# Seven products for eight in three quarters of an encoder's MLP, one core of a Trainium2 chip

## The chip, the core and the metric

The kernel runs on one core of a Trainium2 chip. The metric is the time of one execution on the device in microseconds (us). TensorE (PE) multiplies matrices into the banks of PSUM, VectorE (DVE) and ScalarE (ACT) work on tiles of 128 partitions, GpSimd (POOL) helps, and SyncE (SP) issues transfers (DMA).

## What is computed

Two layers of an encoder on 512 tokens of 1024 features, all in fp32:

```python
for l in range(DEPTH):
    sh1, sc1, gt1, sh2, sc2, gt2 = split(silu(c) @ ada_w[l] + ada_b[l], 6)
    h = rms_norm(x, norm1_g[l]) * (1.0 + sc1) + sh1
    ...
    x = x + gt1 * (merged @ w_out[l])
    h = rms_norm(x, norm2_g[l]) * (1.0 + sc2) + sh2
    x = x + gt2 * (square(relu(h @ w_mlp1[l])) @ w_mlp2[l])
```

What the dots leave out are the two branches of a layer, differential attention and a gated delta rule, with their gates. The last line, the MLP, is what the change is about: `w_mlp1` is 1024 x 4096, `w_mlp2` 4096 x 1024. Both layers have it.

## The kernel before, in words

**Layout.** x and everything dense is feature-major: a tile `xT[k]` holds 128 features (partitions) of all 512 tokens (free dimension), eight tiles for 1024 features. A dense product takes a block of weights of eight 128 x 128 tiles (`chunk`, L539: one load of 1024 values a partition, half a megabyte) and makes 128 output features: the weights stand still in PE, and 512 tokens move.

**Precision.** Every operand of a dense product is a high part, rounded to the format fp32r, and a low part, the difference (`split`, L556). Weights: a cast on ACT (`whi`), a subtraction on DVE (`wlo`), 1024 values a partition each. A product is three passes into one bank: high.high, low.high, high.low. `dense` (L715) does it for all tokens, `dense_halves` (L733) for the first 256 and then the other 256 tokens.

**The MLP** (L1303) goes by quarters of the 4096 hidden features. In each of the four quarters (L1306) the first product makes eight tiles of 128 hidden features: 8 blocks x 8 tiles x 3 passes = 192 matmuls of 512 columns (names `d_m1`; in a layer's first quarter four of the blocks go by halves of the tokens, `d_m1f`). `evac1` (L1309) takes each bank: relu and square on ACT, then the split into `uh` and `ul`. The second product again has 8 blocks x 8 tiles x 3 passes = 192 matmuls (`d_m2`), and `evac2` (L1320) adds each result, times its column of the modulation, to `xT` on DVE. The last quarter of layer 0 goes by halves, since the next layer's norm follows.

**The modulation** (`ada`, L631): each of its 48 columns a layer is a load of half a megabyte and one DVE operation of 1024 values that sums along the row. Those of layer 1 are done beside layer 0's MLP.

**The order.** The code takes operations down (`Plan`, L178); `schedule` (L250) then orders them for each engine by estimated times and five levels (chains, evacuations, weights, dense products, and last what stands beside, such as layer 1's columns), under limits of memory slots, and `issue` (L400) issues them. So every instruction shows line 417, and is known by its tiles. Constants such as the number of slots and of banks kept free stand at L421 and L465.

Of the kernel before, what the change touches and what calls it, by code (L numbers as in the profile page):

```python
# [10 lines left out]
F32 = mybir.dt.float32  # L11
# [17 lines left out]
# columns of the array of vectors  # L29
# [3 lines left out]
# columns of the constant array  # L33
# [31 lines left out]
class Tl:  # L65
    """A tile that gets its memory when its first writer is placed."""
# [14 lines left out]
def _rearrange(a, pat, sizes):  # L81
    """einops' rearrange of a numpy view, for splits, permutations and merges."""
# [27 lines left out]
class View:  # L110
    """A part of a tile: its extent as a numpy view, and the steps that lead to it."""
# [69 lines left out]
class Plan:  # L181
    """Takes down the operations of the kernel in program order, gives them an order by estimated times under the
    limits of memory, and issues them in it."""
# [11 lines left out]
    def add(self, engs, fn, args, kw):  # L195
# [14 lines left out]
        for w, vs in ((False, ins), (True, outs)):  # L210
            for v in vs:
# [20 lines left out]
        # VectorE and GpSimd take turns at their second port to SBUF  # L232
# [6 lines left out]
    def held(self, blocked, order):  # L239
        """What waits for memory, and what holds it."""  # L240
# [8 lines left out]
    # ------------------------------------------------------------------ order  # L249
    def schedule(self):  # L250
# [19 lines left out]
        def offer(op):  # L270
            """Memory for the op, if there is; then it is a candidate from its earliest time."""
# [42 lines left out]
        while todo:  # L314
# [28 lines left out]
            if e != "sp" and op.key[0] >= 0 and HOLD[int(op.key[0])] is not None:  # L343
                # not in the way of a more pressing operation that is about to be ready
# [6 lines left out]
            # two engines don't read one bank of PSUM at the same time  # L351
# [7 lines left out]
            if e == "pe":  # L359
                # TensorE's clock is halved after a window with little work  # L360
# [38 lines left out]
    # ------------------------------------------------------------------ issue  # L399
# [20 lines left out]
# estimates of times in ns, for the order alone  # L420
# [48 lines left out]
# the pieces of the two branches of each layer, in order: d projections of the delta rule, a b c its three parts,  # L469
# z its gate; q k v projections of the attention, t its heads  # L470
# [5 lines left out]
def encoder(ctx, tc, a, out):  # L476
    pl = Plan(tc, {"F": NF, "Y": NY, "Z": NZ, "B": 8},
              {"raw": KRAW, "whi": KHI, "wlo": KLO, "ada0": NADA, "ada": 2, "d": 3, "d0": ND0, "xTp": 1, "po": 2, "pv": 2, "sgf": LSG, "rawg": 1, "whig": 1, "wlog": 1, "dg": 1, "sga": 3, "sc": LSC})
# [24 lines left out]
    # ---------------------------------------------------------------- constants  # L503
# [32 lines left out]
    # ---------------------------------------------------------------- helpers  # L536
    loads = []

    def chunk(src, name, after=(), level=None, cls="F", grp="", wl=2):  # L539
        """A weight block [128, nk, n] of 1024 values a partition, as high and low part: views by k."""  # L540
        nk, n = src.shape[1:]
        per = nk if cls == "F" else nk // 2
        raw = F([P, nk, n], f"raw_{name}", grp="raw" + grp)
        his, los = ([pl.tile(cls, [P, per, n], f"{w}_{name}", F32R, grp=w + grp if cls == "F" else None)
# [16 lines left out]
    def rsqrt(dst, ss, scale):  # L561
        """dst = (ss * scale + eps) ** -0.5: a first guess from the exponent, three Newton steps."""
# [11 lines left out]
    def sumsq(dst, x, by_act):  # L574
        """dst[:, t] = sum of x[:, t]^2 along the row."""
# [10 lines left out]
    def acc(bank, i, lhsT, rhs, stop, level=CHAIN, after=()):  # L586
        """bank[:, i] += lhsT^T rhs: all products into a bank are one group, from the first to the one with stop."""
# [9 lines left out]
    def square(k, xk, hf):  # L597
        """Sums of squares of half of the tokens over the feature tiles of x: a running sum, the last tile for itself."""
# [9 lines left out]
    # ---------------------------------------------------------------- start  # L608
    # twice silu(c), in all partitions
# [6 lines left out]
    # one over the root mean square of x, token-major, on the diagonals of four matrices  # L616
# [33 lines left out]
    for l in range(DEPTH):  # L650
# [6 lines left out]
        # nlam = -(e0 - e1 + lam_init)  # L657
# [75 lines left out]
    def dense_halves(blocks, xh, xl, evac, name, after=()):  # L733
        """Blocks of weights [128, nk, 128], for the first half of the tokens and then for the second; evac(m, psum, half)."""
# [19 lines left out]
    # ---------------------------------------------------------------- the layers  # L754
    mid = []
    for l in range(DEPTH):
# [3 lines left out]
        # ---- per layer constants  # L760
# [19 lines left out]
        # ================================================= differential attention: q, k, v  # L780
# [3 lines left out]
        def da_dense(kind, j):  # L784
            """Columns of one block of two heads, token-major; two banks of two token tiles."""
# [50 lines left out]
        # ================================================= delta rule: projections  # L836
# [36 lines left out]
        # token-major scalars [128, dir, t, h]  # L873
# [4 lines left out]
        def ba_proj():  # L878
            # the high parts of the weights above the low parts: two passes give all products
# [10 lines left out]
            def evac():  # L890
# [9 lines left out]
                # beta = 1 / (1 + exp(-b))  # L900
# [3 lines left out]
                # g = -exp(A_log) * softplus(a + dt_bias)  # L904
# [4 lines left out]
                # log1p(y) = 2 atanh(y / (2 + y))  # L909
# [20 lines left out]
                # the sums as rows  # L930
# [75 lines left out]
            # the 32 x 32 diagonal blocks; partition = (head, unit, block), unit = (dir, chunk)  # L1006
# [21 lines left out]
        def gdn_b(h0, n, XA):  # L1028
            """Inverses of the diagonal blocks of heads h0 .. h0 + n - 1, all at once."""
# [36 lines left out]
            # X = D + N X with N = D L, in three steps; in step n the blocks n beside the diagonal and farther out  # L1066
            # become right, a corner of 4 - n blocks
# [18 lines left out]
            # the recurrence over chunks  # L1086
# [35 lines left out]
            # outputs  # L1122
# [278 lines left out]
```

## Time and profile before

| what | value |
|---|---|
| runs | 1668.42, 1670.18, 1670.42 us, median 1670.18 |
| the profiled execution's span | 1667.5 us |
| PE busy | 1638.8 us (98%), 9456 instructions |
| DVE busy | 1142.1 us (68%) |
| ACT busy | 757.6 us (45%) |
| POOL busy | 159.2 us (10%) |
| DMA | 232.47 MB, mean 139 GB/s |

The span is the profiled execution's own time from its first to its last instruction; the runs are timed by the device from outside, without a profile. Busy time of an instruction goes from its start to its end, and instructions of one engine overlap at their ends, so what one costs in a stream is the distance between two starts. A name such as `d_m` stands for all tiles whose names begin so, and loses its numbers.

### The profile page before, as it was taken

To read this page: it belongs to the slowest core of one execution; us is meant where nothing else is said; L and a number is where in the kernel's file an instruction comes from. 1 tells how busy PE (TensorE), PEld (TensorE's weight loads), DVE (VectorE), ACT (ScalarE), POOL (GpSimd) and SP (SyncE) were. 2 spreads that over 40 slices of the span, in tenths; PEclk is the share of its full clock that TensorE was granted. 3 is DMA by queue.
4 is the path that set the end of the run, shared out by engine and by line. 5 is a ranking of instruction groups with operands and counts; after the bars stand their busy time and mean duration, and the time that the engine had idled before them with its cause. 6 is when DMAs were issued, how large, how long until landed. Compare 5 with 4: busy or idle time off the path is not lost.

```text
span 1667.5 us, 25355 instructions
## 1 busy us (share of the span) xinstructions
PE 1638.8 (98%) x9456; PEld 1410.4 (85%) x9456; DVE 1142.1 (68%) x2653; ACT 757.6 (45%) x1474; POOL 159.2 (10%) x170
## 2 busy tenths in 40 slices
PE   7999999999999999999999999999999999999998
PEld 5889998878898888888998889768889988888887
DVE  7999797898888983333688987998637743333332
ACT  5653452575356252424557335555424652515150
POOL 0231140000300000000023112100002000000000
PEclk9999999999999999999999999999999999999999
DMA  9332534445667982332443332614244433323311
GB/s 379 133 107 96 189 115 146 120 114 186 226 216 265 340 326 90 102 100 90 134 146 113 135 101 72 151 59 126 76 145 139 137 104 101 99 91 101 99 53 51
DMA packets 96782, 232.47 MB, mean 139 GB/s; under 512 B 26625, under 2 KB 37505, under 8 KB 96658
## 3 DMA queue, kind: packets, MB, share of 16 engines
q1 hardware_dynamic: 96658, 230.84, 41.9%
q8 instruction: 74, 1.21, 0.3%
q14 instruction: 50, 0.41, 0.1%
HBM read 217.66 MB, written 13.14 MB: 138 GB/s over the span
## 4 chain that ended last, share of the span: by engine, by line
PE 83%; DVE 12%; DMA 2%; issue 1%; ACT 1%; POOL 0%; SPq 0%; DVEq 0%; ACTq 0%; POOLq 0%
PE d_m L417 39%; PE d_g L417 7%; PE d_dn L417 5%; PE d_out L417 5%; PE d_da L417 5%; PE d_m1f L417 3%; PE d_brb L417 3%; PE d_bra L417 2%; PE d_z L417 2%; PE px L417 2%; PE pv L417 2%; DVE XA L417 2%; DVE btmp L417 2%; PE po L417 1%; PE pog L417 1%
## 5 line engine op out<-in xcount | busy, mean ns | idle before, releaser
L417 PE MATMUL d_m<-uh,wlo_m 128*128 128x512 f32 (+1 forms) x576 | 210.5, 366 | 0.0
L417 PE MATMUL d_m<-ul,whi_m 128*128 128x512 f32 (+1 forms) x576 | 210.4, 365 | 0.0
L417 PE MATMUL d_m<-uh,whi_m 128*128 128x512 f32 (+1 forms) x576 | 210.4, 366 | 0.0
L417 ACT CAST whi_m<-raw_m 128x1024 fp32r<-128x1024 f32 x128 | 132.6, 1049 | 137.1 <-DVE wlo_m L417 70.1
L417 PE MATMUL d_m<-hh,whi_m 128*128 128x512 f32 x448 | 174.3, 389 | 0.0
L417 PE MATMUL d_m<-hl,whi_m 128*128 128x512 f32 x448 | 174.3, 389 | 0.0
L417 PE MATMUL d_m<-hh,wlo_m 128*128 128x512 f32 x448 | 174.3, 389 | 0.0
L417 DVE TENSOR_TENSOR wlo_m<-raw_m,whi_m 128x1024 fp32r<-128x1024 f32 x128 | 156.3, 1221 | 15.8 <-ACT whi_m L417 15.7
L417 DVE SCALAR_TENSOR_TENSOR xT<-d_m,mod,xT 128x512 f32<-128x512 f32 (+1 forms) x72 | 49.7, 690 | 166.5 <-PE d_m L417 166.4
L417 DVE TENSOR_TENSOR ul<-relu,uh 128x512 fp32r<-128x512 f32 x64 | 44.2, 691 | 162.6 <-ACT uh L417 162.6
L417 ACT ACTIVATE relu<-d_m 128x512 f32<-128x512 f32 x56 | 33.5, 598 | 218.8 <-PE d_m L417 218.8
L417 PEld LDWEIGHTS d_m<-ul,whi_m 128*128 128x128 f32 x576 | 108.6, 189 | 17.6
L417 PEld LDWEIGHTS d_m<-uh,wlo_m 128*128 128x128 f32 x576 | 108.6, 189 | 17.5
L417 PEld LDWEIGHTS d_m<-uh,whi_m 128*128 128x128 f32 x576 | 108.6, 189 | 17.4
L417 DVE SCALAR_TENSOR_TENSOR ada<-ada,cb 128x1024 f32<-128x1024 f32 x96 | 116.4, 1227 | 10.0 <-DMA ada<-in_ada_w_dram 8.4
L417 PE MATMUL d_da<-whi_da,hl 128*128 128x256 f32 x384 | 109.4, 287 | 0.0
L417 PE MATMUL d_da<-whi_da,hh 128*128 128x256 f32 x384 | 109.2, 287 | 0.0
L417 PE MATMUL d_da<-wlo_da,hh 128*128 128x256 f32 x384 | 107.5, 287 | 0.0
L417 PE MATMUL d_g<-hh,whi_g 128*128 128x512 f32 x256 | 103.7, 405 | 0.0
L417 PE MATMUL d_g<-hl,whi_g 128*128 128x512 f32 x256 | 103.1, 403 | 0.0
L417 PE MATMUL d_g<-hh,wlo_g 128*128 128x512 f32 x256 | 102.5, 400 | 0.0
L417 PEld LDWEIGHTS d_m<-hh,wlo_m 128*128 128x128 f32 x448 | 84.1, 188 | 17.5
(289 smaller groups left out, 4087.0 us busy)
## 6 DMA issues: line engine op xcount, KB each, us to landing
raw_m<-in_w_mlp_dram SPq DMA_DIRECT2D x128, 512.0 KB, 3.5
ada<-in_ada_w_dram SPq DMA_DIRECT2D x96, 512.0 KB, 6.2
raw_g<-in_w_g_dram SPq DMA_DIRECT2D x32, 512.0 KB, 5.2
raw_out<-in_w_out_dram SPq DMA_DIRECT2D x32, 512.0 KB, 4.3
raw_dn<-in_w_dn_dram SPq DMA_DIRECT2D x24, 512.0 KB, 6.0
raw_da<-in_w_da_dram SPq DMA_DIRECT2D x24, 512.0 KB, 3.9
raw_z<-in_w_dn_dram SPq DMA_DIRECT2D x8, 512.0 KB, 4.9
gb<-grow SPq DMA_DIRECT2D x16, 256.0 KB, 4.7
```

Of the source, the lines that this page charges most:

```text
L417: op.ins = getattr(eng[op.eng[0]], fn)(*[real(v) for v in op.args], **{k: real(v) for k, v in op.kw.items()})
```

## The change

In the first three quarters of each layer (`NSTR = 3`) the second product is cut into blocks, two by two by two: tokens in two halves of 256, the quarter's hidden features into even and odd tiles, output features into two halves of 512. By the scheme of Strassen in Winograd's form seven products of such blocks, with sums of blocks before and after, give what eight products gave. In the sums of u: t1 = o1 - o0 with o0, o1 and so on being pieces of even (e) and odd (o) tiles by halves of the tokens.

- `evac1` makes four differences of 256 tokens for each pair of hidden tiles (`u13`, `u24`) and splits e0 (256) and three tiles of 512 (`ule`, `ul24`, `ul13`, `ulo` are the low parts).
- The weights come in blocks of 512 output features (`load`), are summed in place (`m20` to `m23`, eight sums of 1024 values), and 14 of them are split (`m2hi`, `m2lo`).
- A product (`product`) is token-major: a piece of u stands still, 512 output features of weights move, into a pair of banks for two tiles of 128 tokens: 2 x 4 x 3 = 24 matmuls. Products p1, p6, p7 and p4 add up in one pair (`m2x`), p5 and p3 in another (`m2y`), p2 stands alone (`m2z`).
- `gather` copies or adds these sums into `y`, token-major, 14 times a quarter.
- x is saved to DRAM after the output projection. In the last quarter it is loaded again, y is transposed by PE (32 transposes of 128 x 128 a layer, `yT`), and one DVE operation a tile adds it, times the modulation, to x. The last quarter's second product is done as before.

The diff, cut to its core (comments are dropped throughout the file, and `w_m2` is `w_mlp2` in the new blocks):

```diff
+NSTR, LPLAIN, LSUMS, KEEPS = 3, 8, 8, 1
+G0, G1, G2, G3, G4, G5, GL, GM, GP, GQ = 7, 0, 0, 0, 0, 0, 0, 2, 6, 0
+GS, NYF, KEEPM = (3, 5), 2, (3, 2)
...
             square(m, xT[m], hf)
+            if hf:
+                sp.dma_start(out=xs[m], in_=xT[m], level=SIDE)
...
             def evac1(m, ps):
                 r = Y([P, S], "relu")
                 act.activation(r, ps, AF.Relu)
                 act.activation(r, r, AF.Square)
-                uh.append(Y([P, S], "uh", F32R))
-                ul.append(Y([P, S], "ul", F32R))
-                split(uh[-1], ul[-1], r)
...
+                r0, r1 = r[:, HALF[0]], r[:, HALF[1]]
+                p = m // 2
+                if m % 2 == 0:
+                    split(piece("e0", p, 0), piece("e0", p, 1), r0)
+                    sums = {n: Y([P, 2, S // 2], f"u{n}") for n in ("13", "24")}
+                    minus(sums["13"][:, 0], r1, r0)
+                    even.append((r1, sums))
+                else:
+                    e1, sums = even.pop()
+                    t1, t3, t2, t4 = (sums[n][:, i] for n in ("13", "24") for i in range(2))
+                    minus(t3, r1, e1)
+                    minus(t2, r1, t1)
+                    minus(t4, r0, t2)
+                    sums["o"] = r.rearrange("p (i s) -> p i s", i=2)
+                    for n in ("24", "13", "o"):
+                        split(uP[0][n][p], uP[1][n][p], sums[n])
...
+                for g in range(2):
+                    go = [begin[GS[g]]] + last
+                    a21, a11, a22, a12 = (load(ij, g, go, "sums", KEEPS) for ij in (2, 0, 3, 1))
+                    for dst, x_, y_, o_ in ((a11, a11, a21, ALU.subtract), (a21, a21, a22, ALU.add),
+                                            (a22, a22, a11, ALU.subtract), (a12, a12, a22, ALU.subtract)):
+                        dve.tensor_tensor(out=dst, in0=x_, in1=y_, op=o_, level=WGT)
...
+                p1 = product(plain(0, [begin[GP]] + last), "e0", X, before)
+                gather(X, 0, 0)
+                p6 = product(mixed(s2, [begin[G0]]), "t2", X)
+                gather(X, 0, 1)
+                p5 = product(mixed(s1, [p1[G1]]), "t1", Yq)
+                gather(Yq, 1, 1)
+                p7 = product(mixed(s3, [p6[G2]]), "t3", X)
+                gather(X, 1, 1)
+                p3 = product(mixed(s4, [p5[G3]]), "o1", Yq)
+                gather(Yq, 0, 1)
+                p4 = product(plain(3, [p5[G4]]), "t4", X)
+                gather(X, 1, 0)
+                p2 = product(plain(1, [p7[G5]]), "o0", Z_)
+                gather(Z_, 0, 0)
...
+            for m in range(NK):
+                sp.dma_start(out=xT[m], in_=xs[m], level=WGT, after=before)
+                ps = B([P, S], "yT", grp="m2", keep=KEEPB)
+                for t in range(NT):
+                    pe.transpose(ps[:, t * P:(t + 1) * P], (y[t][:, m // 4] if t < NYF else y[t][m // 4])[:, m % 4 * P:(m % 4 + 1) * P], ident, level=SIDE, after=before)
+                dve.scalar_tensor_tensor(out=xT[m], in0=ps, scalar=mod[l][:, 40 + m:41 + m], in1=xT[m], op0=ALU.mult, op1=ALU.add,
+                                         level=EVAC)
```

The order that this gives, at three places. First VectorE in layer 0, second quarter, at the end of the first product. Before (`ul` is the low part of a hidden tile, `ada1` a column of layer 1's modulation, `wlo_m1` the low part of a weight block of the first product):

```order
L417 TENSOR_TENSOR ul_6741<-relu_6722,uh_6735 128x512
L417 SCALAR_TENSOR_TENSOR ada1_32_6701,mod1_6201<-ada1_32_6701,cb_103 128x1024
L417 SCALAR_TENSOR_TENSOR ada1_33_6713,mod1_6201<-ada1_33_6713,cb_103 128x1024
L417 TENSOR_TENSOR wlo_m15_6765<-raw_m15_6600,whi_m15_6762 128x1024
L417 SCALAR_TENSOR_TENSOR ada1_34_6747,mod1_6201<-ada1_34_6747,cb_103 128x1024
L417 TENSOR_TENSOR ul_6788<-relu_6771,uh_6783 128x512
```

Now, up to the differences of the last pair of hidden tiles:

```order
L417 TENSOR_TENSOR m22_6933<-m22_6933,m23_6944 128x1024
L417 TENSOR_TENSOR ul24_7021<-u24_6995,uh24_7010 128x512
L417 TENSOR_TENSOR m23_6944<-m23_6944,m20_6937 128x1024
L417 TENSOR_TENSOR m21_6971<-m21_6971,m23_6944 128x1024
L417 TENSOR_TENSOR u13_7048<-relu_7032 128x256
L417 TENSOR_TENSOR ule_6959<-relu_7032,uhe_6947 128x256
L417 SCALAR_TENSOR_TENSOR ada1_14_6863,mod1_6475<-ada1_14_6863,cb_103 128x1024
L417 TENSOR_TENSOR m2lo_7065<-m20_6980,m2hi_7024 128x1024
L417 TENSOR_TENSOR m2lo_7076<-m20_6984,m2hi_7037 128x1024
L417 TENSOR_TENSOR u13_7048<-relu_7069,relu_7032 128x256
L417 TENSOR_TENSOR u24_7089<-relu_7069,u13_7048 128x256
L417 TENSOR_TENSOR ulo_7095<-relu_7069,uho_7086 128x512
```

Between two tiles of u there stand sums of weights and pieces of u where there were mostly columns; the last sum (`m21`) comes before the pieces of the last pair.

Then PE in layer 1, second quarter, where the second product passes from its first to its second block. Before (one block of weights to the next, whose results go to another bank):

```order
L417 MATMUL d_m2_15357<-uh_15330,whi_m21_15236 128x512
L417 MATMUL d_m2_15357<-ul_15335,whi_m21_15236 128x512
L417 MATMUL d_m2_15357<-uh_15330,wlo_m21_15239 128x512
L417 MATMUL d_m2_15389<-uh_15064,whi_m22_15274 128x512
L417 MATMUL d_m2_15389<-ul_15069,whi_m22_15274 128x512
L417 MATMUL d_m2_15389<-uh_15064,wlo_m22_15277 128x512
```

Now (from p1's last matmuls to p6's first; `uhe` and `ule` are e0's parts, `uh24` and `ul24` those of t2 and t4):

```order
L417 MATMUL m2x_15788<-m2hi_15738,ule_15655 128x512
L417 MATMUL m2x_15788<-m2lo_15758,uhe_15643 128x512
L417 MATMUL m2x_15763<-m2hi_15727,uh24_15516 128x512
L417 MATMUL m2x_15763<-m2hi_15727,ul24_15521 128x512
L417 MATMUL m2x_15763<-m2lo_15768,uh24_15516 128x512
L417 MATMUL m2x_15763<-m2hi_15727,uh24_15609 128x512
```

The piece of u stands still and the weights move, and p6 goes on in the bank `m2x_15763` that p1 filled 12 matmuls earlier.

Last PE in layer 1, last quarter, after the third block of the second product:

```order
L417 MATMUL d_m2_17068<-uh_17014,whi_m22_16958 128x512
L417 MATMUL d_m2_17068<-ul_17019,whi_m22_16958 128x512
L417 MATMUL d_m2_17068<-uh_17014,wlo_m22_16961 128x512
L417 MATMUL yT_17097<-cst_88,y0_15154 128x128
L417 MATMUL yT_17097<-cst_88,y1_15177 128x128
L417 MATMUL yT_17097<-cst_88,y20_15195 128x128
L417 MATMUL yT_17097<-cst_88,y30_15216 128x128
L417 MATMUL yT_17102<-cst_88,y0_15154 128x128
```

Here nothing stood before between the third and the fourth block; now all 32 transposes do, four into each bank.

## Rows read from the trace of the kernel before

**Rows 1.** The page: span, busy time of each engine, PE's clock in 40 slices

```profile
span 1667.5 us, 25355 instructions
...
PE 1638.8 (98%) x9456; PEld 1410.4 (85%) x9456; DVE 1142.1 (68%) x2653; ACT 757.6 (45%) x1474; POOL 159.2 (10%) x170
...
PEclk9999999999999999999999999999999999999999
```

**Rows 2.** The chain of waits, longest pieces: start us, us, what

```profile
948.52 8.65 PE d_da L417 x72
...
1295.50 16.67 PE d_out L417 x139
...
1336.81 326.44 PE d_m L417 x1440
```

**Rows 3.** Busy time by stage of layer 0's MLP

```profile
core 0: us, PE busy (x) PEld busy (x) DVE busy (x) ACT busy (x) POOL busy (x), PEclk, DMA share, GB/s
497.00:535.50 38.50, 38.50 (x235) 34.51 (x234) 33.73 (x59) 26.41 (x46) 0.00 (x0) 1.00 0.73 254
535.50:579.10 43.60, 43.60 (x194) 36.09 (x193) 39.31 (x62) 10.20 (x11) 0.00 (x0) 1.00 0.95 350
579.10:622.60 43.50, 43.50 (x193) 36.04 (x192) 37.74 (x62) 20.70 (x29) 0.00 (x0) 1.00 0.91 328
622.60:666.00 43.40, 43.40 (x193) 35.92 (x192) 15.10 (x16) 11.04 (x12) 0.00 (x0) 1.00 0.31 98
666.00:709.60 43.60, 43.60 (x194) 36.12 (x193) 15.31 (x16) 19.64 (x28) 0.00 (x0) 1.00 0.30 97
```

**Rows 4.** Timeline of VectorE in layer 0's MLP: start us, us, what

```profile
497.20 2.08 DVE L417 TENSOR_TENSOR xn<-xT,nrb 128x256 f32<-128x256 f32 x6 [0.42 <-PE nrb L417]
...
533.47 0.69 DVE L417 TENSOR_TENSOR ul<-relu,uh 128x512 fp32r<-128x512 f32 x1
534.07 1.22 DVE L417 SCALAR_TENSOR_TENSOR ada<-ada,cb 128x1024 f32<-128x1024 f32 x1
...
541.39 1.22 DVE L417 TENSOR_TENSOR wlo_m<-raw_m,whi_m 128x1024 fp32r<-128x1024 f32 x1
542.52 0.75 DVE L417 SCALAR_TENSOR_TENSOR xT<-d_m,mod,xT 128x512 f32<-128x512 f32 x1
543.19 1.22 DVE L417 SCALAR_TENSOR_TENSOR ada<-ada,cb 128x1024 f32<-128x1024 f32 x1
```

**Rows 5.** Instruction groups of VectorE, 497 to 622.6 us: busy us, mean ns, idle before

```profile
L417 DVE SCALAR_TENSOR_TENSOR ada<-ada,cb 128x1024 f32<-128x1024 f32 x53 | 63.6, 1220 | 10.0 <-DMA ada<-in_ada_w_dram 8.4 <-PE d_m L417 1.5
```

**Rows 6.** Timeline of ScalarE in layer 1's MLP

```profile
1342.31 0.60 ACT L417 ACTIVATE relu<-d_m 128x512 f32<-128x512 f32 x1 [2.60 <-PE d_m L417]
1342.94 0.63 ACT L417 ACTIVATE relu<-relu 128x512 f32<-128x512 f32 x1
1343.61 0.62 ACT L417 CAST uh<-relu 128x512 fp32r<-128x512 f32 x1
1344.13 1.05 ACT L417 CAST whi_m<-raw_m 128x1024 fp32r<-128x1024 f32 x1
```

**Rows 7.** Timeline of PE around four transposes of layer 1's attention

```profile
1194.28 0.60 PE L417 MATMUL oT<-cst,oa 128*128 128x128 f32 x4
1194.64 0.48 PE L417 MATMUL d_brb<-ybh,wlo_brb 128*128 128x512 f32 x1
1194.95 0.40 PE L417 MATMUL d_brb<-ybh,whi_brb 128*128 128x512 f32 x1
```

**Rows 8.** Busy time in three stretches at the start

```profile
5.00:10.00 5.00, 1.21 (x2) 0.00 (x0) 1.73 (x5) 5.00 (x10) 0.00 (x0) 1.00 1.03 405
10.00:15.00 5.00, 2.12 (x10) 2.12 (x11) 4.36 (x21) 0.13 (x2) 0.00 (x0) 1.00 1.03 407
20.00:25.00 5.00, 4.67 (x19) 3.24 (x18) 5.00 (x12) 3.37 (x6) 0.00 (x0) 0.68 1.03 410
```

**Rows 9.** Busy time over most of layer 1's branches

```profile
900.00:1200.00 300.00, 292.42 (x1934) 250.96 (x1934) 259.52 (x765) 157.15 (x381) 48.53 (x60) 1.00 0.34 98
```

More of the change, by code (lines that the diff above doesn't have):

```diff
@@ L542, in chunk @@
         per = nk if cls == "F" else nk // 2
-        raw = F([P, nk, n], f"raw_{name}", grp="raw" + grp)
-        his, los = ([pl.tile(cls, [P, per, n], f"{w}_{name}", F32R, grp=w + grp if cls == "F" else None)
+        kr, kh = KEEPM if name.startswith("m1") and name[2] != "f" else (0, 0)
+        raw = F([P, nk, n], f"raw_{name}", grp="raw" + grp, keep=kr)
+        his, los = ([pl.tile(cls, [P, per, n], f"{w}_{name}", F32R, grp=w + grp if cls == "F" else None, keep=kh)
                      for i in range(nk // per)] for w in ("whi", "wlo"))
@@ L1300, in evac_out, with piece, minus @@
             square(m, xT[m], hf)
+            if hf:
+                sp.dma_start(out=xs[m], in_=xT[m], level=SIDE)
         dense_halves(blocks("w_out", l, NK), mh, ml, evac_out, "out", [gate["a"]])
         h2h, h2l, normed = norm(l, 1, xT)
-        mid = [normed]
+        y, seen, before, late, last = [F([P, 2, 512], f"y{t}") if t < NYF else [Y([P, 512], f"y{t}{i}") for i in range(2)] for t in range(NT)], set(), [], [], []
+        xT = [Y([P, S], f"xT{k}") for k in range(NK)]
         for q in range(4):
-            uh, ul = [], []
+            halves, uh, ul = q < NSTR, [], []
+            if halves:
+                uE = [[Y([P, 2, S // 2], f"{w}e", F32R) for i in range(2)] for w in ("uh", "ul")]
+                uP = [{n: [Y([P, 2, S // 2], f"{w}{n}", F32R) for p in range(4)] for n in ("13", "24", "o")} for w in ("uh", "ul")]
+                place = {"t1": ("13", 0), "t3": ("13", 1), "t2": ("24", 0), "t4": ("24", 1), "o0": ("o", 0), "o1": ("o", 1)}
+            def piece(n, p, w):
+                if n == "e0":
+                    return uE[w][p // 2][:, p % 2]
+                t, i = place[n]
+                return uP[w][t][p][:, i]
+            def minus(dst, x_, y_):
+                dve.tensor_tensor(out=dst, in0=x_, in1=y_, op=ALU.subtract)
             def evac1(m, ps):
@@ L1312, in evac1 @@
                 act.activation(r, r, AF.Square)
-                uh.append(Y([P, S], "uh", F32R))
-                ul.append(Y([P, S], "ul", F32R))
-                split(uh[-1], ul[-1], r)
+                if not halves:
+                    uh.append(Y([P, S], "uh", F32R))
+                    ul.append(Y([P, S], "ul", F32R))
+                    split(uh[-1], ul[-1], r)
+                    return
+                r0, r1 = r[:, HALF[0]], r[:, HALF[1]]
[14 more added lines that the diff above has]
+                        split(uP[0][n][p], uP[1][n][p], sums[n])
@@ L1316, in encoder, with load, parts, product @@
+            even = []
             fresh = 0 if q else FRESH
+            n0 = len(pl.ops)
             dense(blocks("w_mlp1", l, fresh, NK * q), h2h, h2l, evac1, "m1f", fresh=True)
-            dense(blocks("w_mlp1", l, NK - fresh, NK * q + fresh), h2h, h2l, evac1, "m1")
+            dense(blocks("w_mlp1", l, NK - fresh, NK * q + fresh), h2h, h2l, lambda m, ps: evac1(m + fresh, ps), "m1", after=late)
+            begin = [o for o in pl.ops[n0:] if o.eng == ("pe",) and o.kw["start"]]
+            if halves:
+                def load(ij, g, after, grp, keep=0):
+                    t = F([P, 2, 512], f"m2{ij}", grp=grp, keep=keep)
+                    sp.dma_start(out=t, in_=a["w_m2"][l, q, ij, g], level=WGT, after=after)
+                    return t
+                def parts(ts, after, grp):
+                    res = []
+                    for t in ts:
+                        hi, lo = (F([P, 2, 512], f"m2{w}", F32R, grp=w + grp) for w in ("hi", "lo"))
+                        act.copy(hi, t, level=WGT, after=after)
+                        dve.tensor_tensor(out=lo, in0=t, in1=hi.bitcast(F32), op=ALU.subtract, level=WGT)
+                        res.append((hi, lo))
+                    return res
+                def product(A, n, ps, after=()):
+                    ops, done = [], []
+                    for b in range(2):
+                        for p in range(4):
+                            ts = slice(b * P, (b + 1) * P)
+                            g, p2 = p // 2, p % 2
+                            for i, (u_, w_) in enumerate(((0, 0), (1, 0), (0, 1))):
+                                lead = chain.setdefault(id(ps[b].t), [])
+                                mine = [o for o in lead if o in done]
+                                stop = p == 3 and i == 2
+                                op = pe.matmul(ps[b], lhsT=piece(n, p, u_)[:, ts], rhs=A[g][w_][:, p2], start=not lead,
+                                               stop=stop, level=DENSE, skip_group_check=True, after=lead[:1] + (mine if stop else list(after)))
+                                lead.append(op)
+                                done.append(op)
+                                ops.append(op)
+                    return ops
+                def gather(ps, i, th, level=EVAC):
+                    for b in range(2):
+                        dst = y[2 * th + b][:, i] if 2 * th + b < NYF else y[2 * th + b][i]
+                        if (i, th) in seen:
+                            dve.tensor_tensor(out=dst, in0=ps[b], in1=dst, op=ALU.add, level=level)
+                        else:
+                            ad.copy(dst, ps[b], level=level)
+                    seen.add((i, th))
+                def pair(name):
+                    return [B([P, 512], name, grp="m2", keep=KEEPB) for b in range(2)]
+                chain = {}
+                X, Z_, Yq = pair("m2x"), pair("m2z"), pair("m2y")
+                s1, s2, s3, s4 = [], [], [], []
+                for g in range(2):
[4 more added lines that the diff above has]
+                        dve.tensor_tensor(out=dst, in0=x_, in1=y_, op=o_, level=WGT)
+                    s1.append(a21)
+                    s2.append(a22)
+                    s3.append(a11)
+                    s4.append(a12)
+                def plain(ij, after):
+                    return parts([load(ij, g, after, "plain") for g in range(2)], (), "pl")
+                def mixed(ts, after):
+                    return parts(ts, after, "su")
+                p1 = product(plain(0, [begin[GP]] + last), "e0", X, before)
[12 more added lines that the diff above has]
+                gather(Z_, 0, 0)
+                before = p2[-1:]
+                mid = late = p7[GL:GL + 1]
+                last = p4[GQ:GQ + 1]
+                continue
@@ L1329, in encoder @@
             if q == 3 and l + 1 < DEPTH:
-                dense_halves(blocks("w_mlp2", l, NK, NK * q), uh, ul, evac2, "m2")
+                dense_halves(blocks("w_mlp2", l, NK, NK * (q - NSTR)), uh, ul, evac2, "m2", after=begin[GM:GM + 1])
             else:
-                dense(blocks("w_mlp2", l, NK, NK * q), uh, ul, evac2, "m2")
+                dense(blocks("w_mlp2", l, NK, NK * (q - NSTR)), uh, ul, evac2, "m2", after=begin[GM:GM + 1])
     pools = {c: ctx.enter_context(tc.tile_pool(name=f"p{c}", bufs=1, **({"space": bass.MemoryType.PSUM} if c == "B" else {})))
@@ L1356, in layout @@
     da = blocks(w[:, :, 0:OFF_DN], 4, 256)
+    m2 = i["w_mlp2"].reshape(DEPTH, 4, 2, 2, 2, P, 2, 512).transpose(0, 1, 6, 4, 2, 5, 3, 7)
+    m2 = m2.reshape((DEPTH, 4, 4, 2) + m2.shape[-3:])
     res = {
@@ L1373, in layout @@
         "w_mlp1": blocks(i["w_mlp1"], NK, P),
-        "w_mlp2": blocks(i["w_mlp2"], NK, P),
+        "w_mlp2": blocks(i["w_mlp2"], NK, P)[:, NSTR * NK:],
+        "w_m2": m2[:, :NSTR],
         "consts": make_consts(),
```

3 lines of the change are left out of this document (2 added, 1 removed).

## The prediction, on record before the change was run

> **What bounds the kernel now.** First the page's busy shares and its line of clock tenths [rows 1]: TensorE (PE) is busy 1638.8 of 1667.5 us, VectorE (DVE) 1142.1, ScalarE (ACT) 757.6, and no slice has PE's clock under nine tenths. So the time is PE's time, unless another engine starves it somewhere. The chain of waits says what a product costs: in the last stretch 1440 matmuls of 512 columns follow each other in 326.44 us, 0.2267 us each, and a run of 256 columns takes 0.120 us a matmul, whether the weights move (d_da) or the activations do (d_out) [rows 2]. Then the busy times by stage of layer 0's MLP: PE has no gap in any of them, DVE is busy 33.7, 39.3 and 37.7 us in the first three stages (products one, two, one: 125.6 us), then 15.1 and 15.3 in the next two [rows 3]. The first three are full because VectorE also computes layer 1's modulation there, 53 columns of 1.22 us [rows 5]. So there is room for more VectorE work, unevenly: much in layer 1, which has no columns left to compute, less in layer 0.
>
> DVE's own pace, start to start [rows 4]: 1024 columns 1.13 us (541.39 to 542.52), an update of xT by 512 columns 0.67, a difference of 512 columns 0.60, and 256 columns 0.347 (2.08 for six).
>
> **What the change removes.** In each of six quarters (three a layer) the second product had 8 blocks x 8 tiles x 3 passes = 192 matmuls of 512 columns; now 7 products x 2 token tiles x 4 tiles x 3 passes = 168. That is 6 x 24 = 144 fewer. The operands change places (weights move, pieces of u stand still), and by the equal 0.120 us of the two orders at 256 columns [rows 2] I keep the price: 144 x 0.2267 = **-32.6 us**, all of it on PE, which is the path.
>
> **What it adds on PE.** 32 transposes a layer into eight banks, placed together in the last quarter after three blocks of the second product. The trace has four such transposes between other matmuls: from the first to the next matmul's start 0.36 us, and that matmul takes 0.31 to the next start [rows 7] instead of 0.23 [rows 2]. Per layer 8 x 0.36 + 0.08 = 3.0. VectorE empties a bank in 0.67 [rows 4] while PE fills one in 0.36, so towards the eighth bank PE may wait: eight banks filled need 2.9 us, and three are emptied by then, so the wait is small; I add 0.5. If PE had to go at the pace of emptying, 8 x 0.67 = 5.4. Bounds 3.0 to 5.4, taken 3.5 since the row shows the same operation: **+7.0** for two layers (6.0 to 10.8).
>
> By the Trainium skill ("TensorE: Matmul & The Clock Gate", Part 4: PE-mode transpose) a transpose took about 275 ns in one kernel; end on end 64 of them would be 17.6 us and the sum 10.6 us worse. The trace's starts lie 0.09 apart [rows 7], so I let the starts decide.
>
> **What it adds on DVE.** Per quarter before: 16 low parts of weights (16 x 1.13), 8 of u (8 x 0.60), 8 updates of xT (8 x 0.67) = 28.2 us; two stages without columns measured 15.1 + 15.3 = 30.4 by durations [rows 3]. After: low parts 8 + 14 and 8 sums, 30 x 1.13 = 33.9; for each of four pairs of feature tiles five operations of 256 columns and three of 512, 4 x (5 x 0.347 + 3 x 0.60) = 14.1; 14 gatherings into y, 14 x 0.60 = 8.4. Sum 56.4, so +28 a quarter. PE needs (192 + 168) x 0.2267 = 81.6 us for a quarter, so in layer 1 DVE is at 69% and I cost the addition at nothing; its cover is PE's stream. Layer 0's first three quarters: 3 x 56.4 = 169, with 38 columns that the new order spreads over them, 38 x 1.22 = 46 [rows 5], and the norm's 16 x 0.347 = 5.5: 221 of PE's 245 us, 90%. The fullest stretch of before carries 110.8 of 125.6 us, 88%, with PE at 38.50 of 38.50, 43.60 of 43.60 and 43.50 of 43.50 [rows 3]. So 90% sustained is just past what is shown to be free; the price is rival 1's.
>
> **ACT and the transfers.** ACT gets 14 casts of weights for 8 in a quarter: 6 x 1.05 more [rows 6], far from full [rows 1]: nothing. Loads go from 16 to 22 a quarter, half a megabyte each; in layer 0's three quarters 66 + 38 columns are about 54 MB in 245 us, 222 GB/s, while rows 3 show 350 carried without a gap: nothing. The cover here is the lead of the loads, which the order gives out a stage ahead; without it a product of 5.4 us waits for its weights. Saving x after the output projection and loading it again in the last quarter is 32 transfers of 0.26 MB off the path; they stand on SP's queue among loads that are early, nothing.
>
> **Handovers.** A second product now begins with the piece e0 of all tiles, and its second part (t2) needs the differences of the last pair, which exist only after the last block of the first product. The chain after that block: relu 0.60, square 0.63 [rows 6], two differences of 0.35 [rows 4], cast 0.62, low part 0.69: 3.2, and my estimate of 0.5 for four handings on from engine to engine: 3.7 us. In front of t2 lie 24 matmuls, 24 x 0.2267 = 5.4, and nine more before the last pair's piece is read (2.0): 7.5 us of cover. A foreign cast of weights (1.05) on ACT [rows 6] and a low part (1.22) on DVE [rows 4] or two still fit. Before, the last operand took relu, square, cast and low part (2.5) and had 21 matmuls of the first block in front of it, 4.8 us. Bounds 0 and 0.5 us a quarter; I take the middle, **+1.4** for six.
>
> **Layer 1's branches.** The same work stands there in a shuffled order, since the order is planned anew. PE is idle 7.6 of 300 us there (292.42 busy) [rows 9]; the planner could close or double that, so -7.6 to +7.6, taken 0, because every operation and its length is the same.
>
> **The sum.** -32.6 + 7.0 + 1.4 = -24.2 us on the profiled span of 1667.5: 1643.3. The runs' median lies 2.7 above the span: **1646 us**, -1.4%. Its own range is 1638 (branches 7.6 better) to 1651 (0.5 us more of each handover, PE at the pace of emptying, or half of the branches' bad end).
>
> **Rival 1: VectorE becomes the bound in layer 0.** For it: 90% over 245 us, with relu chains and gatherings that must come promptly between 1.2 us weight operations; the new work is in bursts (14.1 us of u and the chain's operations fall in one stage). Against: the planner spread the columns from two stages over seven, and those wait without harm. If only 88% can be used, as the fullest stretch shows, 221 / 0.88 = 251: 7 us lost, about 1653; at 85% 260: 1661. Chance 0.14.
>
> **Rival 2: slower, by a stall at each handover.** If the eight sums of the weights (8 x 1.22 = 9.8 us) stand on VectorE before the last pair's differences, the chain is 3.7 + 9.8 + 2.2 = 15.7 against 7.5 of cover: 8.2 us at each of six starts, 49 in all, less the saving: about 1694. It decides from 4.3 us a handover (25.6 / 6). For it: VectorE takes its work strictly in order, so an early weight sum that waits for a late load holds up all that follows. Against: in the order (the first place shown with the change) two low parts of weights stand ahead of the last pair's differences and none between them, and the sums come before the chain begins. Chance 0.05.
>
> **Rival 3: the clock falls around the transposes.** Trace: after two stretches in which PE was busy 1.21 and 2.12 of 5 us, the granted clock of 20 to 25 us was 0.68 [rows 8]: 3.2 us at 1.2 GHz, 1.6 us lost. If 32 transposes in a row count as little work, each layer loses that: 2 x 1.6 = 3.2, about 1649. The Trainium skill says this of them (the same Part 4: the full clock does not engage for transposes). Against: four transposes among matmuls leave the clock at full [rows 1, 7], but no longer run of them is in the trace that I could set beside 32. Chance 0.05.
>
> **Rival 4: less than it should be, from several small places** (branches at their bad end, last-quarter waits for y or xT): some 1653 to 1668, chance 0.06; "no change" would need 21 us lost of 24, which only this with rival 1 reaches (0.04).
>
> **Chances.** Forecast 0.70, rivals 0.14, 0.05, 0.05, 0.06. A difference under 0.2% (3.3 us) can't be told from none here. Faster: 0.70 + 0.14 + 0.05 + 0.02 = 0.91; same 0.04; slower 0.05. The range reaches from the forecast's low end to rival 1's high end, 1638 to 1661, and leaves out rival 2, most of rival 4 and the forecast's tails.
>
> **What would show it.** PE matmuls of 512 columns still 0.227 apart with u standing still; in the windows of layer 0's MLP PE without a gap while DVE shows near 90%; in layer 1 DVE at about 70%. Each group of 32 transposes takes 3 to 4 us and the clock stays 1.00 beside it. MLP shorter by 16.3 less 3.5 to 4.5 us in each layer, everything else as it was. It is wrong if PE waits on DVE for more than 2 us at the start of t2 or in any stage of layer 0 (rivals 1, 2), or if the branches of layer 1 change by more than 8 us.

## The result, and the profile after

| | before | changed |
|---|---|---|
| runs, us | 1668.42 to 1670.69, median 1670.30 | 1653.88 to 1655.47, median 1655.16 |
| ratio | | 0.991, 95% interval 0.9896 to 0.9924 |
| span of the profiled execution, us | 1667.5 | 1653.7 |

The change makes the kernel faster by 15.1 us. The forecast was 24.2, to 1646; the measured time lies inside the range of 1638 to 1661, but not in the forecast's own range (to 1651). So 9 us are missing. The page of the changed kernel, beside [rows 1]:

```profile
span 1653.7 us, 25702 instructions
...
PE 1618.9 (98%) x9376; PEld 1392.2 (84%) x9376; DVE 1310.5 (79%) x2919; ACT 819.8 (50%) x1572; POOL 162.8 (10%) x170
...
PEclk9999999999999999999999999999999999999999
```

PE is 19.9 us less busy, while the span is only 13.8 shorter. To find the place I cut both spans at the same three events of PE's timeline: the first matmul of layer 0's MLP, its last, the first of layer 1's MLP and the last matmul of all. Busy times in these three stretches, before (columns as in [rows 3]):

```profile
489.52:843.99 354.47, 354.47 (x1845) 305.51 (x1844) 213.81 (x336) 148.02 (x217) 4.48 (x4) 1.00 0.54 188
843.99:1312.01 468.02, 459.97 (x2989) 402.10 (x2988) 373.45 (x1016) 236.14 (x531) 71.94 (x79) 1.00 0.37 114
1312.01:1662.85 350.84, 350.57 (x1642) 294.10 (x1640) 126.31 (x155) 123.88 (x173) 0.00 (x0) 1.00 0.27 88
```

and in the changed kernel:

```profile
488.51:831.56 343.05, 342.68 (x1809) 295.53 (x1807) 299.98 (x469) 181.50 (x268) 4.57 (x5) 1.00 0.64 232
831.56:1311.42 479.86, 464.75 (x2986) 403.92 (x2985) 370.00 (x1014) 234.89 (x531) 75.36 (x78) 1.00 0.35 110
1311.42:1649.52 338.10, 337.83 (x1601) 284.08 (x1600) 211.95 (x290) 153.99 (x220) 0.00 (x0) 1.00 0.37 132
```

Layer 0's MLP is 11.4 us shorter, layer 1's 12.7: together 24.1, as forecast. But layer 1's branches between them, in which the change touches no operation, take 479.86 instead of 468.02 us: **+11.8**. (What is left, 1.5 us, lies before the first cut and after the last.) In the branches PE is idle 15.1 us instead of 8.0.

The MLPs look as the forecast wanted them. Stages of layer 0, first and second products in turn:

```profile
489.00:534.57 45.57, 45.57 (x294) 41.55 (x293) 42.49 (x82) 28.73 (x52) 0.00 (x0) 1.00 0.54 202
534.57:572.60 38.03, 38.03 (x169) 31.51 (x168) 34.60 (x47) 20.40 (x26) 0.00 (x0) 1.00 0.67 237
572.60:616.17 43.57, 43.57 (x193) 36.05 (x193) 36.66 (x56) 22.29 (x34) 0.00 (x0) 1.00 0.65 252
616.17:654.77 38.60, 38.41 (x170) 31.38 (x169) 36.31 (x49) 18.07 (x20) 0.00 (x0) 1.00 0.55 192
654.77:698.29 43.52, 43.52 (x194) 36.04 (x193) 37.54 (x60) 22.28 (x34) 0.00 (x0) 1.00 0.67 252
698.29:736.90 38.61, 38.42 (x170) 31.38 (x168) 36.24 (x48) 18.27 (x21) 0.00 (x0) 1.00 0.57 193
```

VectorE is busy 223.9 of 247.9 us (90%), and PE idles 0.4 us in all six. PE's timeline shows the price of a matmul with u standing still, the wait at a handover, and the transposes:

```profile
550.89 0.39 PE L417 MATMUL m2x<-m2hi,uh 128*128 128x512 f32 x1
551.12 0.39 PE L417 MATMUL m2x<-m2hi,ul 128*128 128x512 f32 x1
...
616.85 0.39 PE L417 MATMUL m2x<-m2hi,ule 128*128 128x512 f32 x1
617.42 0.50 PE L417 MATMUL m2x<-m2lo,uhe 128*128 128x512 f32 x1 [0.18 <-DVE m2lo L417]
...
789.05 3.65 PE L417 MATMUL yT<-cst,y 128*128 128x128 f32 x32
792.47 0.38 PE L417 MATMUL d_m<-uh,whi_m 128*128 128x256 f32 x1
792.69 0.28 PE L417 MATMUL d_m<-ul,whi_m 128*128 128x256 f32 x1
```

Starts lie 0.23 us apart as before. A late low part of weights costs 0.57 - 0.23 = 0.34 us. The 32 transposes take 3.42 us to the next matmul, which takes 0.10 more than the usual 0.12 [rows 2]. The clock beside them:

```profile
789.00:792.50 3.50, 3.50 (x35) 3.50 (x34) 2.81 (x5) 0.00 (x0) 0.00 (x0) 1.00 0.50 201
```

### The profile page after: what moved, and what is told of

Same layout as the page of the kernel before. It is cut to its first block, busy times and chain, and to the rows that moved or that the text cites. A ratio compares the mean times of both kernels' runs of the same rounds, so it can differ in the third digit from the quotient of the medians.

```text
span 1653.7 us, 25702 instructions
## 1 busy us (share of the span) xinstructions
PE 1618.9 (98%) x9376; PEld 1392.2 (84%) x9376; DVE 1310.5 (79%) x2919; ACT 819.8 (50%) x1572; POOL 162.8 (10%) x170
## 4 chain that ended last, share of the span: by engine, by line
PE 79%; DVE 13%; DMA 2%; ACT 2%; issue 2%; SPq 1%; POOL 1%; ACTq 0%; DVEq 0%; POOLq 0%
PE d_m L417 24%; PE m2x L417 8%; PE d_g L417 7%; PE d_out L417 5%; PE d_da L417 4%; PE m2y L417 4%; PE d_dn L417 4%; PE d_m1f L417 3%; PE d_brb L417 3%; PE d_bra L417 2%; PE m2z L417 2%; PE px L417 2%; DVE XA L417 2%; DVE btmp L417 2%; PE pv L417 2%
## 5 line engine op out<-in xcount | busy, mean ns | idle before, releaser
L417 ACT CAST whi_m<-raw_m 128x1024 fp32r<-128x1024 f32 x80 | 83.4, 1048 | 63.7 <-DMA raw_m<-in_w_mlp_dram 47.8
L417 DVE TENSOR_TENSOR wlo_m<-raw_m,whi_m 128x1024 fp32r<-128x1024 f32 x80 | 97.7, 1225 | 16.5 <-ACT whi_m L417 15.1
L417 ACT CAST m2hi<-m 128x1024 fp32r<-128x1024 f32 x84 | 86.5, 1050 | 47.8 <-DMA m<-in_w_m_dram 23.7
L417 DVE TENSOR_TENSOR m2lo<-m,m2hi 128x1024 fp32r<-128x1024 f32 x84 | 99.8, 1219 | 8.2 <-ACT m2hi L417 6.3
L417 PEld LDWEIGHTS d_m<-hh,whi_m 128*128 128x128 f32 x448 | 84.1, 188 | 17.5
L417 PEld LDWEIGHTS d_m<-hl,whi_m 128*128 128x128 f32 x448 | 84.1, 188 | 17.4
L417 PE MATMUL d_dn<-hh,wlo_dn 128*128 128x512 f32 (+1 forms) x208 | 79.1, 383 | 2.5 <-DVE wlo_dn L417 2.5
L417 PE MATMUL d_dn<-hl,whi_dn 128*128 128x512 f32 (+1 forms) x208 | 79.2, 381 | 0.0
L417 PE MATMUL d_dn<-hh,whi_dn 128*128 128x512 f32 (+1 forms) x208 | 77.9, 384 | 0.0
L417 PEld LDWEIGHTS d_da<-whi_da,hh 128*128 128x128 f32 x384 | 73.4, 191 | 0.5
```

What stands on the lines that cost most here:

```text
L417: op.ins = getattr(eng[op.eng[0]], fn)(*[real(v) for v in op.args], **{k: real(v) for k, v in op.kw.items()})
```

## Experiments

**What makes the branches longer.** The order of their 3864 operations is the planner's, drawn up anew for the changed kernel. Theory O: that order is the loss. Rivals: the new MLP leaves something behind that slows the branches (L), or the loss belongs to layer 1's MLP (M). Four runs. The first two write the order down from one kernel and hold the other kernel to it; `REPLAY` is a table of numbers for each engine, taken from the schedule of the other (it also fixes the engine: seven of the operations change between ACT and DVE from one order to the other, so "order" here includes this choice):

```diff
     def schedule(self):
...
+        base = self.mark[0]
+        assert self.mark[1] - base == REPLAYED
+        for e, tab in zip(names, REPLAY):
+            prev = None
+            for k in np.frombuffer(zlib.decompress(base64.b64decode(tab)), np.int16):
+                op = ops[base + int(k)]
+                op.cost, op.eng = [op.cost[op.eng.index(e)]], (e,)
+                if prev is not None and prev.seq not in op.preds:
+                    op.preds[prev.seq] = op.chain = prev
+                prev = op
         for op in ops:
             op.left = len(op.preds)
...
-                at = max([est] + [q.end + lag(q.eng[0], e) for q in op.preds.values()])
+                at = max([est] + [q.start if q is op.chain else q.end + lag(q.eng[0], e) for q in op.preds.values()])
```

The changed kernel in the old order:

> The changed kernel, with layer 1's branches (3864 operations from the norm to the merged branches) held on every engine to the order in which the kernel before issues them. Theory O (the planner's new order of layer 1's branches costs the missing 11.9 us): the branches, from the last matmul of layer 0's MLP to the first of layer 1's, fall from 479.9 back to 468 +- 2 us, time 1655.2 - 11.9 = 1643. Rival L (something that the new MLP leaves behind: memory slots, transfers, the clock): the branches stay at 478 to 481 us, time 1653 to 1657.

The kernel before in the new order:

> The kernel before, with layer 1's branches held to the order of the changed kernel, and nothing else of the change. Theory O: branches 480 us, time 1670.3 + 11.9 = 1682. Rival L: branches stay at 468, time 1670.

The other two give the change to one layer only (`q < NS[l]`, and with it the saving and loading of x, the transposes and the constants):

```diff
+NS = (3, 0)
...
-            halves, uh, ul = q < NSTR, [], []
+            halves, uh, ul = q < NS[l], [], []
```

> Seven products in layer 0 only. The order of layer 1's branches comes out as in the changed kernel on every engine. Theory O: layer 0's MLP gains 11.4 us and the branches lose 11.9: 1670.8, no change that can be measured. Rival M (the loss belongs to layer 1's new MLP, whose loads and slots reach back into the branches): 1670.3 - 11.4 = 1659.

With `NS = (0, 3)`:

> Seven products in layer 1 only. The order of layer 1's branches comes out as in the kernel before. Theory O: branches 468 us, layer 1's MLP 338.1 instead of 350.8: 1670.3 - 12.7 = 1657.6. Rival M: the branches lose 11.9 all the same: 1669.5.

Measured, with the lengths of the three stretches from PE's timeline in one profiled execution each; the ratio is to the kernel before, run beside it:

| kernel | layer 0's MLP | branches | layer 1's MLP | time (median) | ratio, 95% interval |
|---|---|---|---|---|---|
| before | 354.5 | 468.0 | 350.8 | 1669.92 | |
| changed, old order | 343.8 | 469.1 | 338.1 | 1645.97 | 0.9840 to 0.9867 |
| before, new order | 354.5 | 480.6 | 350.9 | 1681.65 | 1.0054 to 1.0082 |
| layer 0 only | 343.1 | 478.3 | 350.8 | 1668.59 | 0.9981 to 0.9998 |
| layer 1 only | 354.5 | 469.0 | 338.1 | 1656.31 | 0.9904 to 0.9929 |

The branches follow the order: 468 to 469 us in the old, 478 to 481 in the new, with either MLP, and holding an order costs 1.1 us at most against the same order left to the planner. L and M are out. Theory O's branches came true within 1.6 us in all four runs; its times were off by up to 3 us (1643 was expected of the first). The held order brings the time that was forecast, and layer 0 alone shows a change that wins 11.4 us and loses 10.3 behind it. The row of the changed kernel's branches in the old order, beside the 464.75 of 479.86 above:

```profile
834.05:1303.19 469.14, 459.33 (x2986) 401.85 (x2985) 372.01 (x1016) 235.30 (x530) 70.58 (x76) 1.00 0.37 113
```

**Is the old order special, or the new one bad?** The planner is greedy, and small changes of its estimates give it another order. Two runs let it draw again:

```diff
+        noise = np.random.default_rng(39).uniform(0, 10, self.mark[1] - self.mark[0])
+        for op, more in zip(ops[self.mark[0]:self.mark[1]], noise):
+            op.cost = [c + float(more) for c in op.cost] if op.eng[0] in ("act", "dve") else op.cost
         for op in ops:
             op.left = len(op.preds)
```

> The changed kernel; the planner's estimates of VectorE's and ScalarE's operations in layer 1's branches get 0 to 10 ns of random surplus each, which changes nothing but the order that it draws up. This draw is the one of 160 whose branches the planner itself holds for shortest: 376.8 us by its estimate, against 382.1 for the changed kernel's order and 375.7 for the order before. Theory P (the loss is a bad draw, and the planner's own estimate ranks the draws): branches 468 to 472 us, time 1643 to 1648. Rival Q (the order before was the product of tuning on the chip, and a fresh draw lands near 480 whatever the planner thinks of it): branches 477 to 485, time 1652 to 1660.

With `default_rng(1)`:

> As the run before, with another draw, an ordinary one (the median of 40 draws with this surplus is 388 us by the planner's estimate, this one has 388.1). Theory P: branches 6 to 12 us longer than in the changed kernel, 486 to 492, time 1661 to 1667. Rival Q: 477 to 485, time 1652 to 1660.

Measured: branches 472.4 us and 1648.44 us (ratio 0.9857 to 0.9890) for the first, 485.5 us and 1661.28 (0.9934 to 0.9964) for the second. The first is 0.4 us over both ends that theory P gave, and Q, which put it at 477 or more, is out. The second does not tell them apart: its branches are half a us under P's and half a us over Q's, its time lies in P's range. The planner's estimate ranks the four orders as the chip does (375.7, 376.8, 382.1 and 388.1 by the one; 468, 472, 480 and 485 by the other), but its differences are too small at the low end, and the last place rests on the clock (last section). So, by the planner's own estimate, the order of before was a rare one, better than all 160 draws, and the new one better than most; on the chip only two draws were measured.

**Is it one late operation?** The longest new wait in the changed kernel's branches is on PE at 914 us:

```profile
913.81 0.60 PE L417 MATMUL qkT<-cst,rot 128*128 128x128 f32 x4
916.94 0.79 PE L417 MATMUL d_dn<-hh,wlo_dn 128*128 128x512 f32 x1 [2.53 <-DVE wlo_dn L417]
917.53 0.63 PE L417 MATMUL d_dn<-hh,whi_dn 128*128 128x512 f32 x1
917.95 0.63 PE L417 MATMUL d_dn<-hl,whi_dn 128*128 128x512 f32 x1
```

VectorE has L and a convolution in front of that low part of weights:

```profile
911.09 2.15 DVE L417 SCALAR_TENSOR_TENSOR L<-kk,gsL,w 128x128 f32<-128x128 f32 x8
913.37 0.75 DVE L417 SCALAR_TENSOR_TENSOR cacc<-d_dn,cols,cacc 128x510 f32<-128x510 f32 x1
...
915.66 1.22 DVE L417 TENSOR_TENSOR wlo_dn<-raw_dn,whi_dn 128x1024 fp32r<-128x1024 f32 x1
```

After the wait PE's matmuls are 0.42 apart instead of 0.23: the granted clock of 916.56 to 921.56 us is 0.66, that is 5 x 0.34 = 1.7 us lost. I moved that operation ahead of L, by one number of VectorE's table of the changed kernel's own order (834, from place 259 to 240). In a second run it stands at place 232, and the next low part (868) goes from 263 to 240:

> The changed kernel with its own order of layer 1's branches held, but for one VectorE operation of 973: the low part of the delta rule's weights (wlo_dn) that PE waits 2.53 us for at 914 us, and after which the clock falls (1.7 us more), is put 19 places earlier, ahead of the eight L operations; its high part has been there since 897 us. Theory V (a few such places cost the 11.9 us, each by its own wait): the wait and the fall of the clock go, branches 479.9 - 4 = 476, time 1651. Rival W (VectorE is the bound over the whole stretch; what is moved ahead delays the chain behind it by its own 1.2 us, and the wait comes back elsewhere): branches 479 to 483, time 1654 to 1658.

> The same with the next block's low part (wlo_dn, 917.6 us) put ahead too, two operations moved. Theory V: the same 4 us less, as PE did not wait for the second. Rival W: 480 to 484, time 1655 to 1659.

Measured: branches 483.1 us, 1659.56 us (ratio 0.9925 to 0.9948), and 480.9 us, 1659.64 us (0.9928 to 0.9952; its profiled execution took 3 us less than its median). Theory V is out: neither run is faster than the changed kernel, whose ratio is 0.9896 to 0.9924. Rival W holds for the branches but for 0.1 us; its times, at most 1658 and 1659, were 1.6 and 0.6 too short. With one moved, the wait for wlo_dn is gone, and a longer one stands 4 us later:

```profile
918.15 0.39 PE L440 MATMUL d_dn<-hh,wlo_dn 128*128 128x512 f32 x1
923.89 1.11 PE L440 MATMUL tokT<-cst,kqv 128*128 128x128 f32 x4 [5.35 <-DVE kqv L440]
```

There VectorE is the bound (busy 5.00, 4.97 and 4.97 us of 5 from 910 to 925). In the changed kernel it already had the moved operations ahead of kqv, so moving them does not bring kqv sooner. With two moved, kqv comes when it came in the changed kernel, and PE, which got its low parts early, has to wait for it. The changed kernel, then two moved:

```profile
920.69 0.68 DVE L417 SCALAR_TENSOR_TENSOR kqv<-kqv,cacc 128x512 f32<-128x512 f32 x1
921.60 0.60 PE L417 MATMUL tokT<-cst,kqv 128*128 128x128 f32 x4
```
```profile
920.56 0.69 DVE L440 SCALAR_TENSOR_TENSOR kqv<-kqv,cacc 128x512 f32<-128x512 f32 x1
921.30 0.66 PE L440 MATMUL tokT<-cst,kqv 128*128 128x128 f32 x4 [2.14 <-DVE kqv L440]
```

With one moved, kqv starts 2.5 us later (923.15). About 2 of these come from three operations of 4 columns ahead of L, which took 0.23 (two) and 0.16 us in the changed kernel and take 1.10 and 1.26 here, beside two operations of GpSimd; no run shows why (the DVE lines, then GpSimd's):

```profile
912.60 1.10 DVE L440 SCALAR_TENSOR_TENSOR gsL<-gsv,rqk 128x4 f32<-128x4 f32 x2
913.62 1.26 DVE L440 TENSOR_SCALAR qal<-rqk 128x4 f32<-128x4 f32 x1
```
```profile
911.69 1.92 POOL L440 TENSOR_TENSOR tok<-tok,gs 128x512 f32<-128x512 f32 x1 [5.93 <-issue]
913.57 1.28 POOL L440 TENSOR_TENSOR rot<-rot,dt 128x512 f32<-128x512 f32 x1
```

So the 11.8 us are not repaired at their widest gap. Of them 7.1 are more idle time of PE and 1.7 the lower clock; the rest, 3.0, is in no wait that the profile lists, and where it lies is not shown.

**How near VectorE is to being the bound in the MLP.** The forecast took VectorE's work for free below PE's time, by sums over a quarter. In layer 1's MLP I computed each low part of the second product's weights twice, then thrice (only this loop differs):

```diff
-                        dve.tensor_tensor(out=lo, in0=t, in1=hi.bitcast(F32), op=ALU.subtract, level=WGT)
+                        for again in range(2 if l else 1):
+                            dve.tensor_tensor(out=lo, in0=t, in1=hi.bitcast(F32), op=ALU.subtract, level=WGT)
```

> The changed kernel, each low part of the second product's weights computed twice on VectorE in layer 1's first three quarters (42 operations of 1024 columns more, 14 a quarter; the order of the branches is as in the changed kernel). VectorE's work rises from about 58.5 to 74.5 of 81.6 us a quarter (91%), and in the stage of the second product from 29.6 to about 45 of 38.1. Theory A (a quarter's sum counts, as in the prediction: under PE's time it is free): layer 1's MLP 338.1 + 0 to 2 us, time 1655 to 1657. Rival S (the stage counts, since the weights can't be made ready a stage ahead): 45 - 38.1 = 7 us in each of three quarters, MLP 359, time 1676.

> As the run before, each low part three times (84 operations more): VectorE 90.5 of 81.6 us a quarter, 61 of 38.1 in the second product's stage. Theory A: 9 us in each quarter, MLP 338.1 + 27 = 365, time 1682; what exceeds that is the share of VectorE's time that can't be used. Rival S: 61 - 38.1 = 23 us in each of three quarters, MLP 407, time 1724.

Measured: 1663.44 us (ratio 0.9951 to 0.9977), MLP 345.9, that is +7.8; and 1707.61 us (1.0212 to 1.0243), MLP 391.0, +52.9. Neither theory's numbers: A gave 0 to 2 and 27, S 21 and 69. The second quarter's second product, first in the changed kernel, then with the low parts computed twice and thrice:

```profile
1439.40:1477.50 38.10, 38.10 (x169) 31.55 (x169) 29.62 (x35) 17.73 (x20) 0.00 (x0) 1.00 0.48 166
```
```profile
1441.00:1483.80 42.80, 41.11 (x176) 32.13 (x175) 42.66 (x48) 17.32 (x19) 0.00 (x0) 1.00 0.41 132
```
```profile
1453.30:1513.40 60.10, 47.88 (x176) 34.08 (x175) 59.84 (x63) 18.25 (x20) 0.00 (x0) 0.91 0.32 103
```

VectorE is busy 42.66 of 42.80 and 59.84 of 60.10 us: it limits the stage, as S has it, and it does so at over 99%, not at the 88% that rival 1 feared. For this stage S was near (45 and 61 us). Over three quarters it gave too much: the first quarter's stage is shorter (40.3 and 54.1 us, 1358.3 to 1398.6 and 1357.9 to 1412.0), and PE has 176 instructions in the stage for 169, since matmuls of the next quarter's first product fill part of the waits. So the stage counts more than the quarter, softened by what PE can move across its ends. In layer 0 the second products stand at 36.3 of 38.6 us: the change had about 2 us a stage to spare there.

## Why the prediction was right or wrong, point by point

- **144 matmuls at 0.2267:** right; matmuls with u standing still have the same spacing.
- **Transposes, +7.0 for two layers:** 3.42 + 0.10 = 3.5 us a layer, as forecast, but by two errors that cancel. The transposes start (3.65 - 0.27) / 31 = 0.109 us apart, not 0.09: the 0.36 of [rows 7] already held three such steps and a short one to the matmul behind. And the 0.5 for a wait at the banks was not needed; PE does not wait there. The figure of the Trainium skill ("TensorE: Matmul & The Clock Gate", Part 4: PE-mode transpose), about 275 ns, laid end on end, would by estimate have given 8.8 us a layer. The trace agrees with it as the duration of one transpose, a median of 273 ns, but the starts lie closer:

```profile
L417 PE MATMUL yT<-cst,y x64: 270/273/275, 789.1 to 1622.4; 128*128 128x128 f32 x64
```

- **Rival 3** did not occur: the granted clock is 1.00 over the 32 transposes in both layers (789.00 to 792.50 above, 1619.00 to 1622.40 in layer 1). The same section of the Trainium skill says that the full clock does not engage for transposes; this run inside a busy stream does not bear that out.
- **Handovers, +1.4:** near in size, but not by the mechanism forecast. PE waits in two of the six, 0.34 and then 0.11 us each, 0.9 in all, both for a low part of the first block's weights (`m2lo`, 617.42 above). At t2, where the chain of the last pair was priced, the profile lists no wait of PE; the 0.5 us for handing on from engine to engine is shown by no row. **Rival 2** did not occur.
- **VectorE in layer 0 at 90%, price nothing:** right; 90% and 0.4 us of PE idle. **Rival 1** did not occur, though its doubt about work that falls in one stage was sound: the doubled low parts limit a stage when the quarter's sum still fits. In layer 1 VectorE is busy 58.5 of 81.6 us a quarter, 72% for the 69 of the forecast.
- **MLP shorter by 12 us a layer:** right, 11.4 and 12.7; of the 1.3 between them 0.9 are the two waits in layer 0.
- **Layer 1's branches, taken 0 with bounds of 7.6 either way "because every operation and its length is the same":** this step failed. They cost 11.8 us, outside its bounds. The length of operations says nothing of their order, and PE's idle time before [rows 9] bounds only what a new order can gain, not what it can lose. By the planner's own estimate the order before was better than any of 160 draws, so another draw was likely to be worse, and the bounds should have been lopsided, from a gain of some us to a loss of 17. The two redraws and the new order give that scale: branches of 472 to 485 us for 468.
- **The range** held the time by luck, through rival 1's end, which did not occur; the forecast's own range took in only half of the branches' bad end. What occurred is the loss that rival 4 named first, at a chance of 0.06, and it was larger than the bad end that it reckoned with. The point named as proof of error, branches that change by more than 8 us, is the one that came true.

## What to carry to other kernels

Where a planner or a scheduler draws up the order of the whole program, an edit in one stage redraws all later stages, and their times are part of what is measured. Compare the stretches that the edit doesn't touch, between the same events of both traces, before the edit is judged; if they differ, hold them to the old order, which here gave 9 us more (1645.97 us, the shortest median of all kernels tried). And count an engine's load by the stage in which its work must be done: what was 91% of a quarter by estimate was over 99% of the stage that waited.

## What was not expected of the hardware

One wait of PE of 2.53 us was followed by matmuls at 1.2 GHz (0.42 us apart) for about 3 us. In the run with two operations moved, waits of 1.70 and 2.14 us left the granted clock at 1.00. PE's timeline and the windows of that run:

```profile
915.52 0.66 PE L440 MATMUL qkT<-cst,rot 128*128 128x128 f32 x4 [1.70 <-POOL rot L440]
...
921.30 0.66 PE L440 MATMUL tokT<-cst,kqv 128*128 128x128 f32 x4 [2.14 <-DVE kqv L440]
```
```profile
912.00:917.00 5.00, 3.30 (x18) 2.46 (x17) 5.00 (x20) 1.87 (x3) 2.32 (x3) 1.00 0.04 7
917.00:922.00 5.00, 2.86 (x15) 2.15 (x14) 4.93 (x11) 0.64 (x2) 1.16 (x4) 1.00 0.52 142
```

So a wait of 2.14 us cost its own length there, and one of 2.53 us cost 2.53 + 1.7 = 4.2. Length alone does not tell which: in the ordinary redraw (e6) the clock fell soon after a wait of 1.72 us, granted 0.66 from 986.60 to 991.60 us:

```profile
985.43 1.10 PE L420 MATMUL pn<-DT,L 128*128 128x96 f32 x8 [1.72 <-DMA DT<-scrT]
```
```profile
986.60:991.60 5.00, 5.00 (x34) 4.36 (x32) 2.23 (x4) 1.62 (x4) 0.00 (x0) 0.66 0.47 121
```

In that run the lower clock took 10.3 of the 17.5 us by which the branches are longer (summed over windows of 5 us). Without the lower clock, by estimate, its branches would take 485.5 - 10.3 = 475.2 us and those of the changed kernel 479.9 - 1.7 = 478.2: on the chip it is the clock that puts the ordinary redraw last. And VectorE can be kept busy at over 99% of a 60 us stage.
